# Four more column tiles of the input projection with tokens on the partitions, and PE transposes for the short convolution

## The chip, the cores and the metric

One core of one Trainium2 chip runs the program. The metric is the device time of one execution in microseconds (us), the median of several runs. The other numbers come from one profiled execution of the same program.

## What is computed

One layer of a decoder for 256 positions (T) and 2048 channels (D), in float32. From h = RMSNorm(x) one wide projection makes the inputs of three token mixers (attention, short convolution, state-space scan) and three merge gates:

```
h = rms_norm(x, g_mix)
... = split(h @ w_in)                       # q, k, v, gate_b, gate_c, u, z, xbc, dt, gm
y_a = nsa_mixer(...)                        # attention
y_b = gate_b * causal_depthwise_conv(gate_c * u, w)    # width 3 over positions
y_c = ssd_mixer(...)                        # state-space scan
gm = sigmoid(gm)
merged = gm[0] * y_a + gm[1] * y_b + gm[2] * y_c
x = x + merged @ w_o
x = x + relu(rms_norm(x) @ w_up) ** 2 @ w_down
x = x + (p @ w_ple) * sigmoid(rms_norm(x) @ w_ple_gate)
out = rms_norm(x, g_final)
```

The change touches y_b and its gate gm[1]: gate_c, u, gate_b and gm[1] are called cc, cu, cb and g1 in the kernel.

## The kernel before

The program is one long stream of weights. All weights stand in DRAM as 686 pieces of 128 x 1024 floats in the order of their use. For each piece SP issues a load into `raw` (6 buffers, line 75), ACT makes a rounded high part (line 87), DVE the low part by subtraction (line 88), both in `w` (4 buffers), and PE multiplies. The activations have a high and a low part too, so each product is three matmuls (high x high, high x low, low x high; `mm3`, lines 171 to 173).

A *unit* is 512 output columns: 8 pieces and 16 row tiles of 128, for all 256 tokens. `unit` (line 914) knows two kinds:

- kind A: tokens on the partitions of the result. The transposed activation tile (128 x 128) is the loaded operand, 512 columns of the weight stream past it. 2 token tiles x 16 row tiles x 3 = 96 matmuls of 512 columns. The two accumulators are [128 tokens, 512].
- kind B: channels on the partitions of the result. A 128 x 128 block of the weight is the loaded operand, the 256 tokens stream past it. 4 blocks x 16 x 3 = 192 matmuls of 256 columns. The accumulators are [128 channels, 2 blocks, 256 tokens].

In the loop over the units of the input projection (from line 964) `A = name in (...)` (line 979) picks the kind. After nine early units, four rounds j = 0 to 3 follow, one for each 512 channels: g0, q, x, z, g2, cc, cu, cb, g1. Of these q, x, z and g2 are of kind A, and g0, cc, cu, cb and g1 of kind B. ACT takes a finished unit out of PSUM (`evac`, line 950); only cu is taken by DVE, which multiplies it with cc on the way (line 1025) into `u`.

What the mixers do besides is cut into jobs: generators that issue a few instructions and then yield their estimated cost in ns. After each piece `side.run(BUDGET)` (line 946) lets the first four jobs in the list take at most one step each, out of a credit of 1200 ns a piece (capped at two pieces' worth). `lag()` gives up two such slots, so that data asked for by PE is ready when PE comes to it. The jobs of a round are `attn_job` (pushed after q), `ssd_job` (after x) and `sconv_job` (after cu); so the short convolution runs while cb and g1 are multiplied, and its last part, which needs g1, falls into the next round's g0, or, in the last round, into the output projection. PE runs its instructions in the order in which the planner of the program has put them; DVE and ACT likewise.

`sconv_job` before (line 893): per block of 128 channels one multiplication and two multiply-adds over shifted tokens (lines 897 to 900), into `yb`; a product with cb over 128 x 1024 (line 905); then `merge` (line 634) with g1 for all 256 tokens: twice a product (line 650) and an addition into `mg` (line 651) over 128 x 512. `mg[j]` is the merged activation, channels on the partitions, as the output projection wants it. `transpose4` (line 427) is four PE transposes of 128 x 128 blocks into one PSUM bank (line 431); attention and the scan use it already. PSUM has four banks for accumulators and four (`s`) for all side work.

The output projection follows (four units of kind A, named by n). `before_wo` splits `mg[c]` into `mTh` and `mTl` ahead of its chunk c; ahead of chunk 3 it lets all jobs come to their end (line 1071). Then come the MLP (16 units of kind B for w_up, 16 of kind A for w_down) and the gated embedding.

Of the kernel before, what the change touches and what calls it, by code (L numbers as in the profile page):

```python
# [21 lines left out]

# w_in column offsets
C_Q, C_KC, C_VC, C_KS, C_VS, C_KW, C_VW = 0, 2048, 2560, 3072, 3584, 4096, 4608
C_GN, C_CB, C_CC, C_CU, C_Z, C_X = 5120, 5168, 7216, 9264, 11312, 13360
C_B, C_C, C_DT, C_GM = 15408, 15920, 16432, 16464

# 1 / 10000 ** (2 i / 128) in float32
INV_FREQ = [
# [9 lines left out]

# 1 / (2 pi) in parts of 12 bits  # L40
TURN = [0.1591796875, -2.4750828742980957e-05, 6.421032594516873e-09,
# [6 lines left out]
def _units():  # L48
    """The column tiles of w_in in the order in which they are multiplied."""
    u = [("kc", 0, C_KC), ("ks", 0, C_KS), ("vs", 0, C_VS), ("kw", 0, C_KW), ("vw", 0, C_VW),  # L50
         ("vc", 0, C_VC), ("small", 0, 0), ("B", 0, C_B), ("C", 0, C_C)]
    for j in range(4):
        o = 512 * j
        u += [("g0", j, C_GM + o), ("q", j, C_Q + o), ("x", j, C_X + o), ("z", j, C_Z + o),
              ("g2", j, C_GM + 4096 + o), ("cc", j, C_CC + o), ("cu", j, C_CU + o),
              ("cb", j, C_CB + o), ("g1", j, C_GM + 2048 + o)]
    return u


def _pieces(name):  # L60
    """Widths of the pieces of a unit; the compression's first layer comes in between B's and C's."""
    return [128] * 2 if name == "small" else [512, 512, 128] * 4 if name in ("B", "C") else [512] * 8


class Stream:
    """Weights in order, two row tiles at a time: loads ahead, then high and low parts ahead of the products."""

# [24 lines left out]
    def get(self, i):  # L92
        """Piece i: [partition, part, row tile, column]."""
        self.convert(i + 1)
        return self.parts.pop(i)


class Side:
    """Work between the main products: each job does at most one step in a slot, a few jobs at a time."""

# [24 lines left out]
    def finish(self, *names):  # L125
        """Bring the named jobs to their end (all of them by default)."""
        while any(not names or n in names for _, n, _ in self.jobs):
            for job in self.jobs[:self.width]:
                self._step(job)


def _kern(tc, xT, xn, pT, pos, wbig, consts, colp, rowp, w2p, normg, gfin, cw, out):
# [50 lines left out]

    # ---- the stream of weights, in the order of their use
    units = _units()
# [19 lines left out]

    # ---- first loads; products on zeros until the first weights are there
    zero = tt([128, 512], name="zero")
# [48 lines left out]

    # ---- transposed activations x g in two parts (the token's factor comes after the first products)
    def aT(name):
# [11 lines left out]
    def rsqrt(dst, ss, n, count):  # L270
        """dst = (ss / count + EPS) ** -0.5 on [128, n]: a first guess from the exponent, three Newton steps."""
        v = sm([128, n], name="v")
# [84 lines left out]

    # ---- scratch in DRAM
    scr = {}
# [4 lines left out]

    # ---- kept over the token mixers
    # keys of a group: [second half, first half] of the selected branch, compressed, window branch
    kT = [kv([128, 2, 528], R32, name="kT") for _ in range(4)]
    vv = {(b, m): kv([128, 2, 512], R32, name="vv") for b in range(2) for m in range(2)}
    K_AT = {(0, 1): 0, (0, 0): 128, (1, 0): 272, (1, 1): 400}
    # compressed branch, 32 rows a part: values [high, high, low], weights [high, low, high]  # L370
    vcg = cst.tile([128, 4, 128], R32, name="vcg")
# [11 lines left out]

    # ---- the token's factor into the activations, once it is known
    hN = []
# [28 lines left out]

    # ---- side jobs
    def rope(dst, src, m):
        """dst, src: [128, 4, 2, 64]"""
        t = tt([128, 4, 2, 64], name="rt")
        V.tensor_tensor(dst, src, bc(cosT[:, m, None, None, :], [128, 4, 2, 64]), OP.mult)
        for h in range(2):  # L420
            V.tensor_tensor(t[:, :, h], src[:, :, 1 - h], bc(sinT[:, m, h, None, :], [128, 4, 64]), OP.mult)
        V.tensor_tensor(dst, dst, t, OP.add)
# [4 lines left out]
    def transpose4(src):  # L427
        """[128, 4 x 128] -> PSUM, each block transposed."""
        p = ps()
        for g in range(4):  # L430
            PE.transpose(p[:, sl(g)], src[:, sl(g)], ident)  # L431
        return p
# [23 lines left out]
    def conv_x(j, dst):  # L456
        """Causal depthwise convolution of the token-major columns kept in scr[j], and SiLU."""
        for hf in range(2):
# [19 lines left out]
    def conv_t(dst, accs, w):  # L478
        """The same with channels on the partitions, from PSUM: dst [128, 4, T], w [128, 4, taps + 1]."""
        for s in range(4):  # L480
# [82 lines left out]
    def blk_job(which):  # L563
        """Blocks of keys (values) with their position codes, transposed: per position [high 64 | low 64]."""
        pe = (pe_k, pe_v)[which]
# [15 lines left out]
    def phi_piece(which, c):  # L581
        """One quarter of the first layer of the compression: all products of the parts in one pass."""
        w = both()
# [50 lines left out]
    def merge(j, dst, a, b):  # L634
        """merged (transposed) += a * b, or a alone."""
        m = tuple(sorted(dst))
# [21 lines left out]
    def attn_job(j, ev):  # L658
# [18 lines left out]
        def pv(m, v, p):  # L677
            """ot[m] += v^T p, all heads at once."""
            if m not in ot:
# [10 lines left out]
        def scores(m, kind, hs):  # L690
            """Products of the queries of heads hs with the keys: one bank."""
            qh, ql = qq[m]
# [6 lines left out]
        def softmax(m, kind, hs, p, e):  # L699
            """e [128, rows, keys]: the gated weights of heads hs."""  # L700
            nr, nk = e.shape[1], e.shape[2]
# [23 lines left out]
        def spread(m, kind, u, p):  # L725
            """The transposed weights of two heads into [keys, part, head, token]."""
            if (m, kind) not in pt:
# [164 lines left out]

    def sconv_job(j, u):
        yb = b4([128, 4, T], name="yb")
        for s in range(4):
            w = scw[:, 4 * j + s]
            V.tensor_scalar(yb[:, s], u[:, s], w[:, 2:3], None, op0=OP.mult)
            for i in range(1, 3):
                V.scalar_tensor_tensor(yb[:, s, i:], u[:, s, :T - i], w[:, 2 - i:3 - i], yb[:, s, i:],
                                       op0=OP.mult, op1=OP.add)  # L900
            if s % 2:
                yield 1700
        while j not in cbe:
            yield None
        V.tensor_tensor(yb, yb, cbe[j], OP.mult)
        yield 1150
        while j not in sig1:
            yield None
        merged(j)
        merge(j, [0, 1], yb, sig1[j])  # L910
        yield 2400

    # ---- main products
    def unit(kind, lhs, accs, before=None, after=None, apart=False):
        """kind A: accs[m] [tokens, 512]; kind B: accs[s // 2] [128 columns, s % 2, tokens]."""
        for c in range(4):
# [3 lines left out]
            if apart and c == 3:  # L920
                # the last three pieces, the first token tile before the second
                w = [(2, 1, last3)] + [(3, hf, piece()) for hf in range(2)]
# [41 lines left out]
    for name, j, _ in units:  # L964
        if name == "small":
# [12 lines left out]
            continue  # L978
        A = name in ("kc", "ks", "vs", "kw", "vw", "q", "x", "z", "g2")
        early = name in ("kc", "ks", "vs", "kw", "vw")  # L980
# [40 lines left out]
        if name == "cu":  # L1021
            u = b4([128, 4, T], name="u")
            with tc.high_priority(offset=1000):
                for i in range(2):
                    V.tensor_tensor(u[:, sl(i, 2)], accs[i], cce[j][:, sl(i, 2)], OP.mult)
            side.push(sconv_job(j, u))
# [38 lines left out]

    # ---- output projection and residual
    mTs = {}
# [8 lines left out]
    def norm_T(n, gains, dst, parts):  # L1076
        """Sums of squares and the transposed, scaled activations of column tile n of x1."""
        h, lo = aT("h2h"), aT("h2l")
# [16 lines left out]
    for n in range(4):  # L1095
        accs = [acc(), acc()]
        # the slots of the merged activations come free chunk by chunk in the last tile
        unit("A", mTs, accs, before=before_wo if n == 0 else None,
# [5 lines left out]

    # ---- MLP, a quarter of the hidden features at a time; the square of the token's factor comes last
    h3, ss3 = {}, cst.tile([128, 2, 4], F32, name="ss3")
# [39 lines left out]

    # ---- per-layer embedding, gated
    pp = {}
# [70 lines left out]
class _Drain:  # L1219
    """Parts that jobs have yet to write: the jobs come to their end when a part is missing."""  # L1220

# [9 lines left out]
def _pack(w, c0, n=512):  # L1231
    """[K, N] -> pieces of [128, 2, 512] (partition, row tile, column)."""
    k = w.shape[0] // 256
# [80 lines left out]
```

## Time and profile before

| | |
|---|---|
| median of 3 runs | 2029.76 us (2028.83 to 2033.18) |
| profiled execution, first to last instruction | 2031.0 us |
| PE busy with matmuls | 2007.7 us, 99% |
| PE weight loads busy | 1821.4 us, 90% |
| DVE busy | 1324.7 us, 65% |
| ACT busy | 1022.5 us, 50% |

The profile gives no time of its own for the profiled execution other than this span; it lies between the fastest and the slowest of the three runs.

Line numbers are those of the kernel before. In the views an instruction's operands are named output<-inputs, where for PE the streamed operand comes first: `acc<-w,hNh` is kind A, `acc<-hNh,w` kind B. "x96" is a count. PE's durations overlap, because matmuls are pipelined: the duration of one is longer than the distance from its start to the next one's start. The times of PE are therefore best read from distances of starts, or from the length of a stretch and the number of matmuls in it.

### The profile page before, as it was taken

To read this page: it belongs to the slowest core of one execution; us is meant where nothing else is said; L and a number is where in the kernel's file an instruction comes from. 1 tells how busy PE (TensorE), PEld (TensorE's weight loads), DVE (VectorE), ACT (ScalarE), POOL (GpSimd) and SP (SyncE) were. 2 spreads that over 40 slices of the span, in tenths; PEclk is the share of its full clock that TensorE was granted. 3 is DMA by queue.
4 is the path that set the end of the run, shared out by engine and by line. 5 is a ranking of instruction groups with operands and counts; after the bars stand their busy time and mean duration, and the time that the engine had idled before them with its cause. 6 is when DMAs were issued, how large, how long until landed. Compare 5 with 4: busy or idle time off the path is not lost.

```text
span 2031.0 us, 31972 instructions
## 1 busy us (share of the span) xinstructions
PE 2007.7 (99%) x12693; PEld 1821.4 (90%) x12693; DVE 1324.7 (65%) x2075; ACT 1022.5 (50%) x1363; POOL 69.7 (3%) x93
## 2 busy tenths in 40 slices
PE   9999999999999999999999999999999999999997
PEld 7899988998799989998899889989988998998886
DVE  7877767766777668766887665555554555555665
ACT  7556556454555455454656454434443443445554
POOL 1000000000000000000000000000000000000011
PEclk9999999999999999999999999999999999999999
DMA  9556666655665566655675555555555555565553
GB/s 334 187 185 208 198 206 199 200 176 182 200 198 193 176 207 203 198 172 194 205 238 178 185 178 181 189 195 187 181 192 193 181 188 196 187 200 191 183 190 107
DMA packets 110277, 393.08 MB, mean 194 GB/s; under 512 B 12628, under 2 KB 13012, under 8 KB 110128
## 3 DMA queue, kind: packets, MB, share of 16 engines
q1 hardware_dynamic: 103552, 368.71, 55.4%
q0 software_dynamic: 6576, 22.34, 3.8%
q8 instruction: 99, 1.62, 0.3%
q14 instruction: 50, 0.41, 0.1%
HBM read 386.75 MB, written 4.25 MB: 193 GB/s over the span
## 4 chain that ended last, share of the span: by engine, by line
PE 51%; DVE 1%; issue 0%; ACT 0%; DMA 0%; POOLq 0%; POOL 0%; ACTq 0%
PE acc L173 17%; PE acc L171 17%; PE acc L172 17%; PE s L431 1%; DVE w L88 0%; DMA cv<-scrx 0%; PE s L171 0%; PE s L173 0%; PE s L172 0%; ACT w L87 0%; PE s L850 0%; ACT L720 0%; ACT scr L1190 0%; POOLq L1307 0%; DVE x L1188 0%
## 5 line engine op out<-in xcount | busy, mean ns | idle before, releaser
L88 DVE TENSOR_TENSOR w<-raw,w 128x1024 fp32r<-128x1024 f32 x686 | 840.1, 1226 | 605.5 <-ACT w L87 603.1
L87 ACT ACTIVATE w<-raw 128x1024 fp32r<-128x1024 f32 x686 | 726.0, 1059 | 850.5 <-PE acc L173 712.5
L171 PE MATMUL acc<-hNh,w 128*128 128x256 f32 x1488 | 423.6, 285 | 0.0
L173 PE MATMUL acc<-hNh,w 128*128 128x256 f32 x1488 | 421.0, 283 | 0.0
L172 PE MATMUL acc<-hNl,w 128*128 128x256 f32 x1488 | 420.9, 283 | 0.0
L171 PE MATMUL acc<-h2h,w 128*128 128x256 f32 x1024 | 290.0, 283 | 0.0
L173 PE MATMUL acc<-h2h,w 128*128 128x256 f32 x1024 | 289.8, 283 | 0.0
L172 PE MATMUL acc<-h2l,w 128*128 128x256 f32 x1024 | 289.8, 283 | 0.0
L172 PEld LDWEIGHTS acc<-hNl,w 128*128 128x128 f32 x1488 | 285.4, 192 | 0.7
L171 PEld LDWEIGHTS acc<-hNh,w 128*128 128x128 f32 x1488 | 285.3, 192 | 0.7
L173 PEld LDWEIGHTS acc<-hNh,w 128*128 128x128 f32 x1488 | 285.3, 192 | 0.0
L171 PE MATMUL acc<-w,hNh 128*128 128x512 f32 x512 | 201.3, 393 | 0.0
L171 PE MATMUL acc<-w,acth 128*128 128x512 f32 x512 | 199.8, 390 | 0.0
L173 PE MATMUL acc<-w,hNl 128*128 128x512 f32 x512 | 199.7, 390 | 0.0
L172 PE MATMUL acc<-w,hNh 128*128 128x512 f32 x512 | 199.5, 390 | 0.0
L173 PE MATMUL acc<-w,actl 128*128 128x512 f32 x512 | 199.3, 389 | 0.0
L172 PE MATMUL acc<-w,acth 128*128 128x512 f32 x512 | 199.3, 389 | 0.0
L172 PEld LDWEIGHTS acc<-h2l,w 128*128 128x128 f32 x1024 | 196.6, 192 | 0.1
L171 PEld LDWEIGHTS acc<-h2h,w 128*128 128x128 f32 x1024 | 196.6, 192 | 0.1
L173 PEld LDWEIGHTS acc<-h2h,w 128*128 128x128 f32 x1024 | 196.6, 192 | 0.0
L173 PEld LDWEIGHTS acc<-w,hNl 128*128 128x128 f32 x512 | 96.1, 188 | 20.6
L173 PEld LDWEIGHTS acc<-w,actl 128*128 128x128 f32 x512 | 96.1, 188 | 20.1
(354 smaller groups left out, 2427.9 us busy)
## 6 DMA issues: line engine op xcount, KB each, us to landing
raw<-wbig SPq DMA_DIRECT2D x686, 512.0 KB, 3.4
cv<-scrx POOLq DMA_DIRECT2D x16, 512.0 KB, 5.9
cw<-cw POOLq DMA_DIRECT2D x8, 512.0 KB, 4.7
E<-acsd POOLq DMA_DIRECT2D x16, 256.0 KB, 4.8
xb<-xn SPq DMA_DIRECT2D x4, 512.0 KB, 9.8
scrx<-ev POOLq DMA_DIRECT2D x4, 512.0 KB, 5.5
x<-xn SPq DMA_DIRECT2D x4, 512.0 KB, 7.1
out<-pp SPq DMA_DIRECT2D x8, 256.0 KB, 2.2
```

The source lines that it names most:

```text
L87: nc.scalar.activation(w[:, 0], s, AF.Copy)
L88: nc.vector.tensor_tensor(w[:, 1], s, w[:, 0].bitcast(F32), OP.subtract)
L171: PE.matmul(o, ah, bh, start=start, stop=False)
L172: PE.matmul(o, ah, bl, start=False, stop=False)
L173: PE.matmul(o, al, bh, start=False, stop=stop)
L431: PE.transpose(p[:, sl(g)], src[:, sl(g)], ident)
```

## The change

cc, cu, cb and g1 become units of kind A in all four rounds (16 units). Their results then have tokens on the partitions. `u` = cu x cc is made there, as two products over 128 x 512 from PSUM, as before. `sconv_job` then

- waits two slots, transposes u with PE, 4 blocks for each of the two token tiles, and has ACT copy them from PSUM into `uT`; the convolution into `yb` then runs as before, on `uT`;
- waits for both cb and g1, multiplies them with each other in place, 128 x 512 for each token tile, waits two slots, transposes the product with PE, and merges with `yb`: the transposed product is read from PSUM, and the merge is made by token tile.

The product of yb with cb over 128 x 1024 is gone.

The diff, without the removed comments and docstrings:

```
     def sconv_job(j, u):
+        uT = b4([128, 4, T], name="uT")
+        yield from lag()
+        for m in range(2):
+            p = transpose4(u[:, m])
+            S.activation(uT[:, :, sl(m)], p.rearrange("p (k t) -> p k t", k=4), AF.Copy)
+            yield 600
         yb = b4([128, 4, T], name="yb")
         for s in range(4):
             w = scw[:, 4 * j + s]
-            V.tensor_scalar(yb[:, s], u[:, s], w[:, 2:3], None, op0=OP.mult)
+            V.tensor_scalar(yb[:, s], uT[:, s], w[:, 2:3], None, op0=OP.mult)
             for i in range(1, 3):
-                V.scalar_tensor_tensor(yb[:, s, i:], u[:, s, :T - i], w[:, 2 - i:3 - i], yb[:, s, i:],
+                V.scalar_tensor_tensor(yb[:, s, i:], uT[:, s, :T - i], w[:, 2 - i:3 - i], yb[:, s, i:],
                                        op0=OP.mult, op1=OP.add)
             if s % 2:
                 yield 1700
-        while j not in cbe:
-            yield None
-        V.tensor_tensor(yb, yb, cbe[j], OP.mult)
-        yield 1150
-        while j not in sig1:
+        while j not in cbe or j not in sig1:
             yield None
         merged(j)
-        merge(j, [0, 1], yb, sig1[j])
-        yield 2400
+        for m in range(2):
+            t = cbe[j][:, m]
+            V.tensor_tensor(t, t, sig1[j][:, m], OP.mult)
+            yield 700
+            yield from lag()
+            p = transpose4(t)
+            merge(j, [m], p.rearrange("p (k t) -> p k t", k=4), yb[:, :, sl(m)])
+            yield 1500
...
-        A = name in ("kc", "ks", "vs", "kw", "vw", "q", "x", "z", "g2")
+        A = name not in ("vc", "B", "C", "g0")
...
         if name == "cu":
-            u = b4([128, 4, T], name="u")
+            u = b4([128, 2, 512], name="u")
             with tc.high_priority(offset=1000):
-                for i in range(2):
-                    V.tensor_tensor(u[:, sl(i, 2)], accs[i], cce[j][:, sl(i, 2)], OP.mult)
+                for m in range(2):
+                    V.tensor_tensor(u[:, m], accs[m], cce[j][:, m], OP.mult)
             side.push(sconv_job(j, u))
```

## Rows read from the trace of the kernel before

**Rows 1.** The page: the span, the engines with busy time, share of the span and number of instructions, and the chain of work that ended last, by engine.

```profile
span 2031.0 us, 31972 instructions
...
PE 2007.7 (99%) x12693; PEld 1821.4 (90%) x12693; DVE 1324.7 (65%) x2075; ACT 1022.5 (50%) x1363; POOL 69.7 (3%) x93
...
PE 51%; DVE 1%; issue 0%; ACT 0%; DMA 0%; POOLq 0%; POOL 0%; ACTq 0%
```

**Rows 2.** The view of waits for PE alone, whole span: who waited for what, us in total, times, longest in us.

```profile
PE s L431 <- DVE mx L718: 5.2, 5, 2.7
...
PE s L171 <- ACT e L720: 1.7, 4, 0.4
...
PE s L431 <- DVE y L885: 0.3, 1, 0.3
```

**Rows 3.** The view of waits for all engines: ACT's conversion of weights, the longest wait of all.

```profile
ACT w L87 <- PE acc L173: 712.5, 413, 3.2
```

**Rows 4.** The view of stretches: two units of kind A (w_down) and two of kind B (w_up) in the MLP, where PE has no side work. Columns: the stretch in us, its length, busy time and count of each engine, granted clock of PE, share of the DMA engines, GB/s. A stretch's count takes in one matmul that runs over its start (two in kind B).

```profile
1492.65:1514.41 21.76, 21.76 (x97) 18.02 (x96) 11.13 (x11) 8.49 (x8) 0.00 (x0) 1.00 0.59 194
1514.41:1536.17 21.76, 21.76 (x97) 18.02 (x96) 11.13 (x11) 8.49 (x8) 0.00 (x0) 1.00 0.59 193
1580.97:1604.01 23.04, 23.04 (x194) 23.04 (x193) 12.30 (x12) 10.59 (x13) 0.00 (x0) 1.00 0.55 183
1604.01:1627.05 23.04, 23.04 (x194) 23.04 (x193) 12.30 (x12) 10.60 (x13) 0.00 (x0) 1.00 0.55 184
```

**Rows 5.** The same view, unit by unit, columns as before: x and g2 of round 1; cc, cu, cb and g1 of round 1; g0, q and x of round 2; and the first unit of the output projection.

```profile
479.73:502.45 22.72, 22.72 (x105) 18.80 (x104) 14.76 (x18) 10.55 (x13) 0.00 (x0) 1.00 0.58 186
...
530.88:558.54 27.66, 27.26 (x136) 22.66 (x135) 23.43 (x65) 17.58 (x33) 2.27 (x3) 1.00 0.60 200
558.54:586.32 27.78, 27.78 (x222) 27.18 (x221) 21.72 (x37) 14.84 (x19) 2.04 (x3) 1.00 0.65 209
586.32:609.36 23.04, 23.04 (x194) 23.04 (x193) 16.92 (x21) 13.45 (x17) 0.00 (x0) 1.00 0.56 184
609.36:634.17 24.81, 24.81 (x210) 24.81 (x209) 16.91 (x27) 8.98 (x9) 2.03 (x3) 1.00 0.67 213
634.17:658.33 24.16, 24.16 (x201) 24.02 (x200) 19.66 (x40) 15.17 (x21) 0.00 (x0) 1.00 0.52 175
658.33:683.07 24.74, 24.74 (x210) 24.74 (x209) 13.65 (x15) 10.94 (x13) 0.00 (x0) 1.00 0.54 173
683.07:706.17 23.10, 23.10 (x105) 19.06 (x105) 16.10 (x28) 9.45 (x12) 0.00 (x0) 1.00 0.56 180
706.17:728.90 22.73, 22.73 (x105) 18.80 (x104) 14.76 (x18) 10.55 (x13) 0.00 (x0) 1.00 0.57 185
1105.08:1129.38 24.30, 24.30 (x117) 20.37 (x116) 17.11 (x24) 12.15 (x15) 0.55 (x1) 1.00 0.60 196
```

**Rows 6.** The view of line 431, the transposes: its matmuls by what they transpose, their number, and the duration of one in ns (least, median, most). `transpose4` issues four of them at a time.

```profile
L431 PE MATMUL s<-kb,e x96: 270/272/302, 297.0 to 1015.5; 128*128 128x128 f32 x96
...
L431 PE MATMUL s<-kb,x x64: 270/272/273, 1182.2 to 1931.2; 128*128 128x128 f32 x64
...
L431 PE MATMUL s<-kb,qr x32: 270/272/273, 270.0 to 946.5; 128*128 128x128 f32 x32
...
L431 PE MATMUL s<-kb,y x32: 270/272/328, 425.7 to 1134.3; 128*128 128x128 f32 x32
...
L431 PE MATMUL s<-kb,kr x24: 270/272/273, 71.6 to 115.3; 128*128 128x128 f32 x24
```

**Rows 7.** The timeline of PE in unit x of round 2, around four transposes in a row: start in us, duration in us.

```profile
719.78 0.60 PE L431 MATMUL s<-kb,qr 128*128 128x128 f32 x4
720.14 0.48 PE L171 MATMUL acc<-w,hNh 128*128 128x512 f32 x1
720.45 0.40 PE L172 MATMUL acc<-w,hNh 128*128 128x512 f32 x1
```

**Rows 8.** The view of groups by line and form, for the stretch from 456 to 1106 us (rounds 1 to 3): busy time in us, mean ns of one, idle time of the engine before them.

```profile
L163 ACT ACTIVATE pth<-s 128x512 fp32r<-128x512 f32 x18 | 10.5, 583 | 0.0
L855 DVE TENSOR_TENSOR y<-y,s 128x256 f32<-128x256 f32 x22 | 9.2, 417 | 0.3
...
L905 DVE TENSOR_TENSOR yb<-yb,ev 128x1024 f32<-128x1024 f32 x3 | 3.7, 1219 | 0.0
L650 DVE TENSOR_TENSOR mt<-yb,ev 128x512 f32<-128x512 f32 x5 | 3.4, 689 | 1.7 <-ACT ev L957 1.7
...
L651 DVE TENSOR_TENSOR mg<-mg,mt 128x512 f32<-128x512 f32 x4 | 2.8, 689 | 0.1
```

**Rows 9.** The timeline of the end of the last scan job, in the output projection: start in us, duration in us, and in brackets the idle time of the engine before it.

```profile
1133.21 0.69 DVE L885 TENSOR_TENSOR y<-y,ev 128x512 f32<-128x512 f32 x1
...
1133.96 0.66 PE L431 MATMUL s<-kb,y 128*128 128x128 f32 x4 [0.32 <-DVE y L885]
...
1134.96 0.68 DVE L646 TENSOR_TENSOR mg<-mg,s 128x512 f32<-128x512 f32 x1
...
1135.67 1.06 ACT L163 ACTIVATE mTh<-mg 128x1024 fp32r<-128x1024 f32 x1 [2.31 <-DVE mg L646]
...
1136.76 1.23 DVE L164 TENSOR_TENSOR mTl<-mg,mTh 128x1024 fp32r<-128x1024 f32 x1 [1.13 <-ACT mTh L163]
1136.77 0.40 PE L172 MATMUL acc<-w,mTh 128*128 128x512 f32 x1
```

## The prediction

> **What bounds the kernel now.** I began with the page. PE is busy for 99% of the span, and in the chain that ended last PE has 51% where every other engine has 1% or less [rows 1]. A busy PE is no proof, since durations of matmuls overlap, so I asked next who PE waits for. The largest wait between its first matmul and its last is 5.2 us in five places, transposes of attention weights that DVE had not got ready; then 1.7 us in four, and tenths [rows 2]. The view of all waits says the same from the other side: ACT, which makes the weights for PE, waits 712.5 us until PE gives back a weight buffer [rows 3]. So weights are ready ahead of PE, and neither DMA, ACT nor DVE sets the pace. The time is PE's instruction stream, and the question is what a unit of each kind costs there. That is read where nothing else runs on PE, in the MLP: a unit of kind A takes 21.76 us, one of kind B 23.04 us [rows 4]. Both stream 96 x 512 = 192 x 256 = 49,152 columns. Divided by the counts, a matmul of 512 columns takes 226.7 ns and one of 256 columns 120.0 ns, so two of the latter cost 13 ns more. The weight loads show why: in kind B they fill 23.04 of 23.04 us, in kind A 18.02 of 21.76 [rows 4]. The granted clock is 1.00 in all these stretches (the 2.4 GHz level).
>
> **The units that change kind.** Sixteen units (cc, cu, cb, g1 in four rounds) go from B to A: 16 x (23.04 - 21.76) = 20.5 us less. That the MLP's figures hold here too is seen in cu of round 1, which has no side work on PE: it takes 23.04 us, as in the MLP, though DVE works 16.92 us in it. And x, a unit of kind A with 8 transposes in it, takes 22.72 us [rows 5].
>
> **The new transposes.** Each round adds 4 groups of 4 transposes, 16 groups in all. One transpose is recorded with 272 ns, whatever it transposes [rows 6], but they overlap: four together take 0.60 us, and the next matmul starts 0.36 us after the first of them [rows 7]. What a group costs the stream is best read from unit x, which has two groups and nothing else: 22.72 - 21.76 = 0.96 us, 0.48 us a group [rows 4, 5]. In a unit of kind B a group costs less. g1 of round 1 has 4 transposes and 3 products of 512 columns and takes 1.12 us more than 23.04 [rows 5]; without 3 x 0.227 that leaves 0.44. The two groups for u fall into cb (now A), 2 x 0.48. The two for cb x g1 fall into the next g0 (B), 2 x 0.44, in the last round into the output projection (A), 2 x 0.48. Sum: 3 x 1.84 + 1.92 = 7.4 us; bounds 16 x 0.44 = 7.0 and 16 x 0.48 = 7.7. The Trainium skill has a rule that speaks against this (TensorE: Matmul & The Clock Gate, Part 4: PE-mode transpose): about 275 ns for a transpose in a kernel's context, by which the 64 would cost 17.6 us and the gain below would shrink to a fraction of a us. The recorded duration agrees with it; the distance of starts does not, and it is the distance that PE's stream pays.
>
> **Side work that now stands in units of kind A.** The matmuls of attention and scan in cc, cb and g1 stay, but around them the form changes. The sixteen in cb (two groups of the scan's) cost 24.81 - 23.04 = 1.77 us; in the first unit of the output projection, of kind A, two such groups and 3 products of 512 columns cost 24.30 - 21.76 = 2.54, without 3 x 0.227 that is 1.86. The seven in g1 cost 1.12, a like seven in q 23.10 - 21.76 = 1.34 [rows 4, 5]. So kind A pays 0.09 us more for two interruptions in the one case and 0.22 in the other. cc has 29 side matmuls, by their number some six interruptions, 0.3 to 0.7 us more by these two. A round: 0.09 + 0.22 + 0.3 to 0.7, together 2.4 to 4.0 us for four. From below 0, if the differences are the transitions between units and not the interruptions. I take 2.0, below the middle of what the rows give, because the 0.22 of q also holds a change of form at its start.
>
> **DVE and ACT.** Per round DVE loses one product of 1.22 us and four of 0.69 us (3.98), and gains two of 0.69 and eight over 256 elements, which in the nearest row (an addition from PSUM) take 0.42 each: 4.7 us [rows 8]. ACT gains two copies from PSUM of 0.58 us. That costs nothing as long as PE has work: in cb and g1 DVE is busy for 16.91 of 24.81 and 19.66 of 24.16 us, ACT for 8.98 and 15.17, and the later g0, where the second part goes, has 13.65 of 24.74 on DVE [rows 5]. A faster stream asks for a piece of weights every 2.72 instead of 2.88 us; the MLP's A units live on that without a wait [rows 4]. The products that make u are the same number over the same size.
>
> **New waits.** PE now waits for u, and for cb x g1, ahead of its transposes; behind a waiting transpose stands the whole stream, and all units with it. The cover is the two slots of `lag`, 2 x 2.7 us, against 0.7 us of DVE work for each tile. ACT's copy and DVE's merges wait for these transposes; behind them stand conversions of weights, and PE would miss those only when it has used up what is converted ahead, and the wait of ACT for free buffers [rows 3] says that it is ahead. I set the waits at 0. From above: the trace has 248 transposes, 62 groups of four [rows 6], and five waits for the maximum and one for y came to 5.5 us [rows 2], 0.09 us a group, 1.4 us for 16. From below: the order of side work shifts, and the five waits of 5.2 us could vanish. No DMA of a side job is added or moved.
>
> **The last round.** Its cb x g1 product, two groups of transposes and merges come into the output projection, where the scan's own end is tight. PE already waited 0.32 us for y there; mTh of the last chunk was ready at 1136.73 us and its matmul started at 1136.77 [rows 9]. Each us that this chain gets longer may cost a us. Before, the short convolution put 2.76 us of DVE work there, early; now it is 4.7 us, of which the second merge (1.7 us) falls among the scan's last steps. DVE is busy for 17.11 of 24.30 us in this unit [rows 5], so part of it goes into gaps. Bounds 0 and 2.0; I take 0.7, nearer to the gaps, since DVE sat idle for 1.13 us inside this very chain.
>
> **Sum.** -20.5 + 7.4 + 2.0 + 0.7 = -10.4 us on a span of 2031.0. That span is 1.2 us above the median of the runs and inside their spread, so I take the difference off the median: 2029.76 - 10.4 = 2019.4.
>
> **Rivals.**
> *The waits of attention go away.* All 5.2 us [rows 2]: 2014.2. For it: the order of the side work shifts. Against it: those transposes stand in z, which the change does not touch.
> *The new groups wait.* Place: PE ahead of the 16 new groups. The price of such a wait is known from attention, 5.2 / 5 = 1.04 us [rows 2]. If each group paid it: 16.6 us, 2036.0, slower than before. It decides from 0.40 us a group on (then the gain is inside 0.2%), and from 0.90 us on the kernel is slower by more than 0.2%. For it: DVE and ACT keep a fixed order, and a late instruction holds up all behind it. Against it: two slots of cover, and only 5 of all earlier groups waited so long. A part of it, or the output projection paying its full 2.0 us and more, gives 2021.5 to 2025.7.
> *Each transpose costs its recorded duration.* 64 x 0.272 = 17.4 instead of 7.4 us [rows 6]: 2029.4, no measurable change. Against it stands unit x [rows 5]. This is what the Trainium skill's figure above would give.
> *The change does not bring the faster form.* If the work of DVE, not PE's columns, set the pace of these units, the 20.5 us would not come, and the rest stays: 2039.9. For it: DVE is busy for 23.43 of 27.66 us in g2, of kind A. Against it: even there PE is busy for 27.26 [rows 5].
>
> **How the numbers follow.** A measurement of this kernel can tell about 0.2%, 4.1 us, from no change, so faster means under 2025.7 and slower over 2033.8. Chances: the sum within some 2 us 0.62; waits of attention gone 0.08; part of the new waits or a late output projection, up to 2025.7, 0.15; these three are faster, 0.85. Waits of 0.40 to 0.90 us a group 0.07 and transposes at full duration 0.03, the same, 0.10. Waits beyond that 0.03 and no faster form 0.02, slower, 0.05. The bounds of the terms give -20.5 + 7.0 + 0 + 0 - 5.2 = -18.7, 2011, and -20.5 + 7.7 + 4.0 + 2.0 + 1.4 = -5.4, 2024.4. All at one end at once is unlikely below, so I take 2012; above, the case of partial waits reaches to 2025.7, so I take 2025. With that less than 2 in 10 is left out: the 0.15 of the last four cases and the rims.
>
> **What the profile after would show.** The units cc, cu, cb and g1 with 96 matmuls of 512 columns each; cu without side work at 21.76 us; cb at about 1.3 us less for its form and 0.96 us more for two groups; weight loads no longer filling these units; g0 longer by 0.9 us; PE's waits still some 5 us, none on transposes of u or of the product; in the output projection the last `mg` about 1 us later. The prediction is wrong if line 431 gets waits of half a us in many places, if cu stays near 23 us, or if conversions of weights appear among PE's waits.

## The result, and the profile after

The changed kernel takes 2019.73 us (median of 4 runs, 2019.0 to 2020.36) where the kernel before takes 2029.49 (4 runs, 2028.83 to 2033.18): a ratio of 0.9949, 95% interval 0.9937 to 0.9961. It is 9.8 us faster; 10.4 had been forecast. The profiled spans differ by more, 2031.0 - 2017.0 = 14.0 us. Wherever a run's time and its span are both on record, the time is 1.8 to 2.5 us longer; so the profiled execution of the kernel before is one of about 2033 us, near the slowest of its runs and some 3.5 us above their median (the prediction compared span and run directly and had 1.2), and that of the changed kernel one of 2019.0, its fastest. What makes executions differ is one of the findings below.

The page of the changed kernel, as in [rows 1]: the span, and the engines' busy time, share and instructions.

```profile
span 2017.0 us, 29062 instructions
...
PE 1995.5 (99%) x11221; PEld 1747.1 (87%) x11221; DVE 1325.3 (66%) x2095; ACT 1024.3 (51%) x1369; POOL 69.5 (3%) x93
```

PE is still busy for 99%, with 1472 matmuls fewer: 16 x 96 went, 64 transposes came. DVE and ACT do what they did.

The view of stretches of the changed kernel, unit by unit as in [rows 5]: x, cc, cu, cb and g1 of round 1, g0 and q of round 2, and the first two units of the output projection.

```profile
476.27:499.00 22.73, 22.73 (x105) 18.80 (x104) 14.76 (x18) 10.54 (x13) 0.00 (x0) 1.00 0.55 186
552.20:578.99 26.79, 26.79 (x127) 22.08 (x125) 21.81 (x37) 14.81 (x19) 2.04 (x3) 1.00 0.64 215
578.99:600.75 21.76, 21.76 (x98) 18.02 (x96) 16.72 (x21) 13.61 (x17) 0.00 (x0) 1.00 0.58 196
600.75:625.31 24.56, 24.56 (x121) 20.59 (x120) 16.89 (x27) 9.94 (x11) 2.03 (x3) 1.00 0.58 190
625.31:648.27 22.96, 22.96 (x105) 18.98 (x103) 18.69 (x40) 15.04 (x21) 0.00 (x0) 1.00 0.61 210
648.27:674.56 26.29, 26.29 (x220) 26.10 (x219) 14.53 (x20) 11.33 (x13) 0.00 (x0) 1.00 0.53 175
674.56:696.93 22.37, 22.37 (x104) 18.51 (x102) 16.37 (x30) 9.33 (x12) 0.00 (x0) 1.00 0.52 172
...
1089.45:1114.69 25.24, 25.24 (x124) 21.16 (x123) 18.95 (x29) 11.23 (x14) 0.55 (x1) 1.00 0.54 175
1114.69:1137.71 23.02, 22.57 (x101) 18.19 (x100) 15.82 (x27) 10.55 (x13) 0.00 (x0) 1.00 0.56 181
```

Read it beside [rows 5]. cu, with no side work on PE, went from 23.04 to 21.76 us, the length of a unit of kind A in the MLP to the hundredth; its weight loads fill 18.02 us and no longer all of it. cc went from 27.78 to 26.79, g1 from 24.16 to 22.96. cb has two groups of transposes more and is still 0.25 us shorter. g0 and q together are 26.29 + 22.37 - 24.74 - 23.10 = 0.82 us longer: two groups in a unit of kind B (three products moved from q to g0 as well). x, untouched, is the same. The output projection's first two units are 25.24 + 23.02 - 24.30 - 22.87 = 1.09 us longer, with two groups in them.

The timeline of PE in cb of round 1, around the first group for u, and the view of PE's waits, both of the changed kernel.

```profile
609.84 0.60 PE L431 MATMUL s<-kb,u 128*128 128x128 f32 x4
610.19 0.48 PE L171 MATMUL acc<-w,hNh 128*128 128x512 f32 x1
```

```profile
PE s L431 <- DVE mx L718: 2.7, 3, 1.3
PE s L171 <- ACT e L720: 1.7, 4, 0.4
...
PE s L431 <- DVE y L885: 0.4, 1, 0.4
```

From the first of the four new transposes to the next matmul it is 0.35 us; attention's took 0.36 [rows 7]. PE's waits are those of before [rows 2], 2.5 us less of them on attention's maximum. None is on u or on the product of cb and g1.

The timeline of the changed kernel at the end of the last scan job, as in [rows 9]: the wait for y, and the last addition into `mg`.

```profile
1119.50 0.63 PE L431 MATMUL s<-kb,y 128*128 128x128 f32 x4 [0.45 <-DVE y L885]
...
1120.41 0.68 DVE L646 TENSOR_TENSOR mg<-mg,s 128x512 f32<-128x512 f32 x1
```

The last `mg` comes 1120.41 - 1089.45 = 30.96 us after the start of the output projection, before it was 1134.96 - 1105.08 = 29.88 [rows 5, 9]: 1.1 us later, of which 0.94 is the longer first unit. PE's wait for y grew from 0.32 to 0.45 us.

The groups by line and form for rounds 1 to 3 of the changed kernel (453 to 1090 us), as in [rows 8]: the merge from PSUM, the copies into uT, the product of cb and g1.

```profile
L650 DVE TENSOR_TENSOR mt<-s,yb 128x256 f32<-128x256 f32 x10 | 3.8, 418 | 2.2 <-PE s L431 2.2
L651 DVE TENSOR_TENSOR mg<-mg,mt 128x256 f32<-128x256 f32 x10 | 3.8, 418 | 0.0
L898 ACT ACTIVATE uT<-s 128x512 f32<-128x512 f32 x6 | 3.5, 580 | 0.0
L914 DVE TENSOR_TENSOR ev<-ev 128x512 f32<-128x512 f32 x4 | 2.8, 688 | 1.2 <-ACT ev L965 1.2
```

These are the prices that were taken from the nearest rows: 0.418 us for 256 elements from PSUM, 0.58 for ACT's copy, 0.69 for the product.

### The profile page after: what moved, and what is told of

Read it like the earlier page. It is cut to its first block, busy times and chain, and to the rows that moved or that the text cites. A ratio compares the mean times of both kernels' runs of the same rounds, so it can differ in the third digit from the quotient of the medians.

```text
span 2017.0 us, 29062 instructions
## 1 busy us (share of the span) xinstructions
PE 1995.5 (99%) x11221; PEld 1747.1 (87%) x11221; DVE 1325.3 (66%) x2095; ACT 1024.3 (51%) x1369; POOL 69.5 (3%) x93
## 4 chain that ended last, share of the span: by engine, by line
PE 51%; DVE 1%; issue 0%; ACT 0%; DMA 0%; POOLq 0%; POOL 0%; ACTq 0%
PE acc L171 17%; PE acc L173 17%; PE acc L172 17%; PE s L431 1%; DVE w L88 0%; DMA cv<-scrx 0%; PE s L171 0%; PE s L173 0%; PE s L172 0%; PE s L850 0%; ACT L720 0%; ACT scr L1198 0%; POOLq L1315 0%; DVE x L1196 0%; ACT w L87 0%
## 5 line engine op out<-in xcount | busy, mean ns | idle before, releaser
L171 PE MATMUL acc<-w,hNh 128*128 128x512 f32 x1024 | 403.9, 394 | 0.0
L173 PE MATMUL acc<-w,hNl 128*128 128x512 f32 x1024 | 399.3, 390 | 0.0
L172 PE MATMUL acc<-w,hNh 128*128 128x512 f32 x1024 | 399.2, 390 | 0.0
L173 PEld LDWEIGHTS acc<-w,hNl 128*128 128x128 f32 x1024 | 192.2, 188 | 41.2
L172 PEld LDWEIGHTS acc<-w,hNh 128*128 128x128 f32 x1024 | 192.5, 188 | 37.2
L171 PEld LDWEIGHTS acc<-w,hNh 128*128 128x128 f32 x1024 | 192.3, 188 | 37.2
L171 PE MATMUL acc<-hNh,w 128*128 128x256 f32 x464 | 132.4, 285 | 0.0
L173 PE MATMUL acc<-hNh,w 128*128 128x256 f32 x464 | 131.3, 283 | 0.0
L172 PE MATMUL acc<-hNl,w 128*128 128x256 f32 x464 | 131.2, 283 | 0.0
L172 PEld LDWEIGHTS acc<-w,acth 128*128 128x128 f32 x512 | 96.2, 188 | 19.6
```

The costliest lines, as they stand in the source:

```text
L171: PE.matmul(o, ah, bh, start=start, stop=False)
L172: PE.matmul(o, ah, bl, start=False, stop=False)
L173: PE.matmul(o, al, bh, start=False, stop=stop)
```

## The experiments

Times of a run are medians. The kernel before, run again beside the experiments, came to 2027.7 to 2035.6 us, with medians of 2029.05 to 2032.4 from batch to batch; the changed kernel was not run again beside them. So differences of a few us are read from the units of the profiles.

**1. No transposes.** In `sconv_job` of the changed kernel:

```
-            p = transpose4(u[:, m])
-            S.activation(uT[:, :, sl(m)], p.rearrange("p (k t) -> p k t", k=4), AF.Copy)
+            S.activation(uT[:, :, sl(m)], u[:, m].rearrange("p (k t) -> p k t", k=4), AF.Copy)
...
-            p = transpose4(t)
-            merge(j, [m], p.rearrange("p (k t) -> p k t", k=4), yb[:, :, sl(m)])
+            merge(j, [m], t.rearrange("p (k t) -> p k t", k=4), yb[:, :, sl(m)])
```

> The changed kernel without its 64 new transposes: ACT copies u straight into uT, and the merge reads the product of cb and g1 from SBUF. Left out: the swap of tokens and channels in the short convolution and its gate, so the values of y_b are others; all other work stays. Theory (each group of four costs PE's stream 0.44 to 0.48 us, and nothing waits for it): 7.4 us under the changed kernel's 2019.73, 2012.3. Rival 1 (each transpose costs its recorded 0.272 us): 17.4 us under, 2002.3. Rival 2 (part of the price of the new groups is waits): more than 8 us under, 2011 or less, and the units that lose their groups get shorter by more than 0.48 us a group.

Measured: 2016.21 us (2015.26 to 2016.71), 3.5 us less and not 7.4: by its time the theory missed. The view of stretches of this kernel, for z of round 1 and cb of round 1:

```profile
497.76:527.82 30.06, 26.30 (x120) 21.68 (x119) 19.10 (x47) 15.47 (x31) 3.12 (x5) 0.94 0.60 193
603.31:626.91 23.60, 23.60 (x114) 19.81 (x112) 16.98 (x27) 10.01 (x11) 2.04 (x3) 1.00 0.73 223
```

cb lost 0.96 us for its two groups, as expected, and over all units that had groups the loss is 7.2 us. But z of round 1, which the edit does not touch, takes 30.06 us instead of 25.51, and PE is busy for only 26.30 of them. The timeline there:

```profile
514.09 1.22 DVE L470 TENSOR_TENSOR cv<-cv,cw 128x1024 f32<-128x1024 f32 x1 [6.35 <-DMA cv<-scrx]
...
516.71 0.16 DVE L718 TENSOR_SCALAR mx<-mx 128x2 f32<-128x2 f32 x1
...
516.93 0.41 PE L431 MATMUL s<-kb,e 128*128 128x128 f32 x2 [1.10 <-DVE mx L718]
520.00 0.66 PE L431 MATMUL s<-kb,e 128*128 128x128 f32 x2 [2.66 <-DVE mx L718]
```

DVE stands for 6.35 us in the first product of the scan's convolution, whose data goes through DRAM and back; behind it, in DVE's fixed order, stands the maximum that attention's weights need, and PE waits for their transposes. The same wait is in z of round 1 of the kernel before, which took 28.42 us:

```profile
518.47 1.23 DVE L470 TENSOR_TENSOR cv<-cv,cw 128x1024 f32<-128x1024 f32 x1 [6.04 <-DMA cv<-scrx]
...
521.32 0.41 PE L431 MATMUL s<-kb,e 128*128 128x128 f32 x2 [0.78 <-DVE mx L718]
524.39 0.41 PE L431 MATMUL s<-kb,e 128*128 128x128 f32 x2 [2.66 <-DVE mx L718]
```

and, shorter, in the changed kernel:

```profile
512.15 1.23 DVE L470 TENSOR_TENSOR cv<-cv,cw 128x1024 f32<-128x1024 f32 x1 [3.16 <-DMA cv<-scrx]
...
518.06 0.41 PE L431 MATMUL s<-kb,e 128*128 128x128 f32 x2 [0.75 <-DVE mx L718]
```

Stretches of 2 us of run 1 show a second price, the granted clock (third column from the right):

```profile
515.00:517.00 2.00, 0.90 (x5) 0.47 (x4) 2.00 (x5) 0.10 (x1) 0.00 (x0) 1.00 0.38 51
...
519.00:521.00 2.00, 0.99 (x5) 1.03 (x6) 2.00 (x7) 1.03 (x5) 0.00 (x0) 0.61 0.51 180
521.00:523.00 2.00, 2.00 (x7) 1.61 (x7) 2.00 (x9) 1.21 (x2) 0.54 (x1) 0.54 0.46 160
```

After PE had been idle for most of 515.8 to 520.0 us, its clock was granted at the lower level (1.2 GHz) for a part of 519 to 523 us, and only 7 matmuls went through in 2 us where 11 do. Runs 8 to 11 follow this up.

**2. Each new transpose twice.** `for g in range(4 * times): PE.transpose(p[:, sl(g % 4)], src[:, sl(g % 4)], ident)` with `times=2` at the two new places.

> The changed kernel with each of its 64 new transposes issued twice in a row into the same bank; the computation is the same. Theory (the distance of starts counts, 0.109 us): 64 x 0.109 = 7.0 us over 2019.73, 2026.7, and cb longer by 2 x 0.44. Rival 1 (the recorded duration counts): 17.4 us over, 2037.1. Rival 2 (PE has slack at these places): under 3 us over.

Measured: 2025.56 us, 5.8 us more where the theory had 7.0. cb of round 1 in the view of stretches:

```profile
603.76:629.15 25.39, 25.39 (x130) 21.47 (x128) 16.88 (x27) 9.94 (x11) 2.04 (x3) 1.00 0.54 177
```

25.39 - 24.56 = 0.83 us for eight more transposes, 0.104 us each, as expected. So PE's stream pays the distance of starts; the recorded 0.272 us would have made 2.2 us of it. That rival falls.

**3 and 4. Each half alone.** First only cc and cu change kind, then only cb and g1:

```
-        A = name not in ("vc", "B", "C", "g0")
+        A = name not in ("vc", "B", "C", "g0", "cb", "g1")     # 3, with the old product and merge
+        A = name not in ("vc", "B", "C", "g0", "cc", "cu")     # 4, with the old u, uT = u
```

> One half of the change: cc and cu of kind A with u transposed, cb and g1 of kind B with the old product and merge. Theory (terms add): cc 0.99 and cu 1.28 us less a round, as the changed kernel's profile has them, 9.1 us in four rounds; 8 groups of transposes in a unit of kind B, 8 x 0.44 = 3.5 us more; 5.6 us under the kernel before, 2023.9. Rival (the two halves help each other, by one shared wait or by the buffers): this half alone gives 3 us or less, 2026.5 or more.

> The other half: cb and g1 of kind A, multiplied with each other and transposed for the merge, cc and cu of kind B with u made with channels on the partitions as before. Theory (terms add): cb 1.2 and g1 1.2 us less a round, 9.6 us in four; 8 groups, 0.82 us a round in g0 and q and 1.1 in the output projection, 3.6 us more; 6.0 us under the kernel before, 2023.5, and with the other half 11.6 us. Rival (the last round's tail and the merge from PSUM eat it): 3 us or less, 2026.5 or more.

Measured: 2022.96 us (2022.15 to 2023.47) and 2026.46 us (2022.54 to 2027.29). The first half is as expected. The second half's median misses, and its runs lie in two bunches, near 2023 and near 2027; the profiled span, 2021.3 us, belongs to the first bunch and its units are those expected. cb and g1 of round 1:

```profile
604.85:628.47 23.62, 23.62 (x114) 19.81 (x113) 16.82 (x27) 8.96 (x9) 2.04 (x3) 1.00 0.68 223
628.47:651.45 22.98, 22.98 (x105) 18.97 (x103) 18.67 (x40) 15.04 (x21) 0.00 (x0) 1.00 0.55 183
```

They are 1.2 us shorter each, and g0 and q are 0.84 us longer together. That the second bunch is the wait in z is not shown, as only one execution has a trace.

**5. No slots of cover.** Both `yield from lag()` in `sconv_job` taken out.

> The changed kernel without the two slots of cover ahead of its 16 groups of transposes: they are asked for right after the products that they turn; the computation is the same. Theory (the new waits are 0 because of the two slots): without them PE waits for DVE at the 8 groups of cb x g1, about as long as attention's waits, 0.5 to 1.0 us each, and not for u, which is ready before the first slot ends: 4 to 8 us over 2019.73, about 2025. Rival (the planner of the order already puts the transposes where their data is ready, and the slots do nothing): within 1.5 us of 2019.73.

Measured: 2019.99 us, the same as with them; the theory missed and the rival held. The timeline of this kernel at cb of round 1:

```profile
600.33 1.28 DVE L1031 TENSOR_TENSOR u<-acc,ev 128x512 f32<-128x512 f32 x2
...
604.10 0.66 PE L431 MATMUL s<-kb,u 128*128 128x128 f32 x4
```

The first group for u comes 3.5 us into cb, with the slots 9.1 us; u is ready 1.0 us into cb in both. The theory spoke of the groups for cb x g1; the first of round 1, in the next g0:

```profile
648.53 0.69 DVE L913 TENSOR_TENSOR ev<-ev 128x512 f32<-128x512 f32 x1 [0.68 <-ACT ev L963]
...
653.75 0.60 PE L431 MATMUL s<-kb,ev 128*128 128x128 f32 x4
```

The product is ready at 649.22 us, and its transposes come 4.5 us later. So without the slots, too, PE's transposes are put behind their data; whether the steps of the jobs or the planner does that was not tested.

**6. Kind A for w_up too.** On top of the changed kernel; w_up's units become "A", and the squared activations are turned in a side job:

```
+        def act_turn(a, n, ts):
+            yield from lag()
+            h, lo = b4([128, 4, T], R32, name="acth"), b4([128, 4, T], R32, name="actl")
+            for m in range(2):
+                p = transpose4(ts[m])
+                split(h[:, :, sl(m)], lo[:, :, sl(m)], p.rearrange("p (k t) -> p k t", k=4))
...
-                unit("B", h2, accs)
+                unit("A", h2, accs)
```

> The same exchange at 16 more units, on top of the changed kernel: the MLP's w_up of kind A, its squared activations transposed by PE in groups of four, two groups a unit, split from PSUM; the computation is the same. Theory (a unit of kind A with two groups costs 21.76 + 0.97 = 22.73 us against 23.04, and the two slots cover the waits): 16 x 0.31 = 5.0 us under 2019.73, 2014.7. Rival (the last unit's activations come late for w_down, or ACT and DVE, which split from PSUM, hold up the weights): each of the four changes from w_up to w_down waits 1.2 us or more, and nothing is gained, 2019.7 or more.

Measured: 2015.5 us (2014.31 to 2016.84), 4.2 us less. Two stretches of this kernel, a unit of w_up and the first of w_down, which now holds the last unit's transposes:

```profile
1252.57:1275.29 22.72, 22.72 (x105) 18.81 (x104) 12.30 (x12) 10.53 (x13) 0.00 (x0) 1.00 0.54 185
1275.29:1298.02 22.73, 22.73 (x105) 18.80 (x104) 12.51 (x13) 10.06 (x12) 0.00 (x0) 1.00 0.54 186
```

22.72 us, as unit x [rows 5], against 23.04 [rows 4]; PE has no wait in either.

**7. The last round's gate as before.** `... and not (j == 3 and name in ("cb", "g1"))`, with the old product and merge in that round.

> The changed kernel, but in the last round cb and g1 stay of kind B with the old product and merge, so that no transposes come into the output projection. Read from the units of the profile. Theory (nothing but columns and groups): cb and g1 of that round 1.2 us longer each, the first two units of the output projection together 1.0 to 1.1 us shorter, mg of the last scan in time as before. Rival (the tail pays for DVE's extra work as well): the output projection gets shorter by 1.7 us or more.

Measured (one run, 2020.28 us): cb and g1 of the last round are 1.1 and 1.2 us longer, and the first two units of the output projection 1.1 us shorter than in the changed kernel:

```profile
1092.25:1116.55 24.30, 24.30 (x117) 20.38 (x116) 17.10 (x24) 12.17 (x15) 0.55 (x1) 1.00 0.57 190
1116.55:1139.40 22.85, 22.54 (x101) 18.24 (x100) 15.71 (x26) 10.56 (x13) 0.00 (x0) 1.00 0.54 179
```

That is two groups at 0.48 and 0.15 us more; DVE's extra work there costs next to nothing.

**8 to 11. The wait in z moved away.** In `conv_x`, DVE's first product of a round goes four slots back (`lag(2)` gives up four; the first expectation counts five), behind the conversion of weights that is due then (`ws.last`, which the stream of weights now keeps):

```
                 yield 0
-                V.tensor_tensor(u, u, w, OP.mult)
+                if hf == 0 and m == 0:
+                    yield from lag(2)
+                    with tc.issue_after(getattr(ws.last, "ins", ws.last)):
+                        V.tensor_tensor(u, u, w, OP.mult)
+                else:
+                    V.tensor_tensor(u, u, w, OP.mult)
```

This was run with the kernel before, with the changed kernel, with run 6 and with run 1.

> The kernel before, with one instruction moved: in each round DVE's first product of the scan's convolution (line 470), which waits for data that goes through DRAM and back, is put five slots later in DVE's order, behind a conversion of weights that is due then; the computation is the same. It tests what sets the spread of unit z, the only unit whose length differs from profile to profile. Theory (DVE stands in that wait, attention's maximum is late behind it, and PE waits for it): DVE's waits for cv fall from 24 us to under 5, PE's waits for line 718 from 5.2 us to under 1, all four z between 24.0 and 25.0 us, and the time 2 to 4 us under the kernel before's. Rival (PE's waits in z come from attention's own chain): z and the time unchanged within 1 us.

> The changed kernel with the same one instruction moved. With z out of the comparison the change alone is left. Theory (the sum of the units' differences in the two profiles, z left out): 11 to 12 us under the run above, a ratio of 0.9943. Rival (what the change gives depends on the waits in z): 9 us or less under it, or 14 or more.

> The changed kernel with w_up of kind A (as in the run of that name) and the same one instruction moved. Theory (terms add): 4.5 to 5.0 us under the run above. Rival (they get in each other's way): 3 us or less under it.

> The changed kernel without its 64 new transposes (left out as in the first experiment, so the values of y_b are others) and with the scan's one instruction moved. The first experiment gained 3.5 us where 7.4 were expected, while the units that lost their groups got shorter by 7.2 us and z of round 1 longer by 4.6. Theory (that z was the same wait for data through DRAM, in an unlucky place): with z out of the way the transposes' price shows in full, 7.2 us under the changed kernel with the moved instruction, 2008.1, and all four z within 0.2 us of 26.2. Rival (without the transposes something else waits in z): z of round 1 stays longer than the others by 2 us or more, and the time is 2010 or more.

| | us, median | lowest to highest | runs |
|---|---|---|---|
| kernel before, moved | 2027.29 | 2026.81 to 2027.87 | 11 |
| changed kernel, moved | 2015.33 | 2015.19 to 2015.57 | 5 |
| and w_up of kind A | 2010.01 | 2009.5 to 2010.17 | 4 |
| changed kernel, no transposes, moved | 2007.81 | 2007.39 to 2008.15 | 4 |

The spread of several us is gone. The four z of the kernel before with the move, in the view of stretches:

```profile
278.44:304.60 26.16, 26.14 (x131) 21.78 (x130) 19.24 (x53) 16.94 (x33) 3.93 (x6) 1.00 0.73 230
500.95:527.23 26.28, 26.28 (x130) 21.81 (x129) 19.27 (x53) 16.93 (x33) 3.89 (x6) 1.00 0.72 230
723.53:749.69 26.16, 26.14 (x130) 21.78 (x129) 19.23 (x53) 16.93 (x33) 3.90 (x6) 1.00 0.73 230
946.05:972.33 26.28, 26.28 (x130) 21.80 (x129) 19.27 (x53) 16.92 (x33) 3.90 (x6) 1.00 0.73 229
```

PE is busy throughout; its waits for line 718 are gone altogether. The four z of runs 9 and 11 are as long, 26.15 to 26.28 us. Three details were expected otherwise: the z are 26.2 us and not 24 to 25, because attention gets further in them (33 side matmuls instead of 22, which later units no longer have), DVE still waits 12.4 us for data from DRAM, in later products, with no wait of PE for line 718 behind them; and the time is 5.1 us under the kernel before's 2032.4 beside it, where 2 to 4 were expected. The move also brought in a new wait of PE, for a conversion of weights in the second unit of the output projection, from the view of PE's waits of run 8:

```profile
PE acc L172 <- DVE w L88: 0.8, 1, 0.8
```

That unit takes 23.70 us in run 8, against 22.87 in the kernel before and 23.01 in run 9. Without the transposes, too, z of round 1 is no longer than the others, and cb is as short as in run 1:

```profile
496.69:522.97 26.28, 26.28 (x131) 21.82 (x130) 19.26 (x53) 16.91 (x33) 3.88 (x6) 1.00 0.71 231
...
597.34:620.94 23.60, 23.60 (x114) 19.80 (x113) 16.97 (x27) 10.01 (x11) 2.03 (x3) 1.00 0.67 223
```

So with the move the change gives 2027.29 - 2015.33 = 12.0 us. Of these, 0.8 is the wait just named, which run 8 has and run 9 has not: the change by itself is worth some 11.2 us, and the two first profiles with z left out say the same, 14.0 - 2.6 = 11.4. The transposes cost 2015.33 - 2007.81 = 7.5 us; run 11 was made on another chip than runs 8 to 10, but units without transposes agree (cu 21.76 us in both), and by the units alone the difference is 7.2 us. w_up of kind A gives another 5.3 us, slightly more than expected. The third row of the table is 0.9896 of the kernel before run beside it, interval 0.9883 to 0.9910.

## Why the prediction came out

*What bounds the kernel, and the form.* Right. PE's instruction stream sets the time, and 512 columns in one matmul are cheaper than in two. cu shows it alone (23.04 to 21.76), and kernel before and run 11, both with z out of the way, differ by 2027.29 - 2007.81 = 19.5 us for the sixteen units with their side work, 0.8 of it the wait in run 8. The rival that DVE's work would keep the units at their old length is refuted: cc has 21.81 us of DVE's work in 26.79 and became 0.99 us shorter. What the prediction gave as the reason, weight loads that fill a unit of kind B, stays open. From the page of the kernel before:

```profile
L172 PEld LDWEIGHTS acc<-h2l,w 128*128 128x128 f32 x1024 | 196.6, 192 | 0.1
```

A load is recorded with 192 ns. At a distance of 120 ns such records overlap and fill the stretch, whatever sets the distance, just as those of the matmuls do; no run tells the two apart.

*The transposes.* Right: 7.4 forecast, 7.2 by the units of runs 1 and 11 and 7.5 by the medians of runs 9 and 11, and the price is the distance of starts. The Trainium skill's figure (TensorE: Matmul & The Clock Gate, Part 4: PE-mode transpose), about 275 ns and given there for bfloat16, is what the trace records for one, 272; as a price in a dense stream it does not hold here, 0.104 us in run 2.

*Side work in units of kind A.* Right: 2.0 us forecast; cc, cb and g1 of the profiles give 0.29 + 0.07 + 0.08 a round, 1.8 in all. The runs with z out of the way give 20.5 - 19.5 = 1.0, and 1.8 once the wait of 0.8 us in run 8 is taken out. Within the term g1's share is 0.08 where q's row had suggested 0.22, of which the prediction itself suspected a part to be q's change of form.

*New waits at 0.* Right in size: the view of waits has none on the new groups. Wrong in its reason: without the two slots there is none either (run 5).

*The last round.* 0.7 us forecast, 1.09 - 0.96 = 0.13 measured, 0.15 by run 7. The last `mg` did come 1.1 us later, as forecast, but nearly all of that is the first unit's own length with its two groups; PE's wait for y grew by only 0.13 us.

*The sum.* With what the units of the profiles show, it is -20.5 + 7.2 + 1.8 + 0.1 = -11.4, and that is the difference of the profiles with z left out. The forecast's -10.4 was 1.0 us short: 0.6 too dear in the last round, 0.2 each in the transposes and the side work. That it lies within 0.6 us of the 9.8 of the medians is partly luck, because the medians hold something that no term contained: the wait in z, which differs from execution to execution (25.2 to 28.4 us for z of the kernel before, 24.9 to 26.0 for the changed one). The same changed kernel stands 9.8 us under the four runs of the kernel before that were made with it, and would stand 12.7 under the median of 2032.4 of the fifteen beside runs 8 to 10. In the two profiled executions z together is 2.6 us shorter, hence 14.0 us there. The rival *waits of attention go away* named this wait but took its row for something fixed; in the profiled executions half of it went (5.2 to 2.7 us), in z, which the change does not touch, and in run 1 it is 5.2 us again.

## What to carry to other kernels

When PE's stream is the bound, count what each form of a product costs there from the start of one matmul to the start of the next, in a stretch without side work, and add the interruptions as the difference of two stretches; durations of single matmuls or transposes mislead by a factor of about two (272 against 104 ns for a transpose). A swap of partitions and columns can pay for its transposes: a unit of kind A with eight of them (22.73 us) was shorter here than one of kind B with none (23.04 us). Before comparing kernels to a few us, look for the one unit that differs from profile to profile and take its cause out of both: here one instruction, put where its data has arrived, made the spread of the kernel before several times smaller (6.9 us in fifteen runs, 1.1 in eleven). And look for what the moved kernel waits for instead: 0.8 of the 12.0 us was such a wait.

## What was not expected of the hardware

A pause of PE can cost more than its own length. In z of round 1 DVE waited for data that goes through DRAM and back, 6.0 us in the kernel before and 6.4 in run 1, and PE was idle for 0.78 + 2.66 and 1.10 + 2.66 us around the same two transposes. In run 1 the granted clock then fell, 0.61 and 0.54 on average over two stretches of 2 us, 7 matmuls ran where 11 do, and PE was busy for 26.30 us in the unit:

```profile
502.46:530.88 28.42, 24.98 (x119) 20.58 (x118) 17.93 (x44) 14.16 (x30) 3.12 (x5) 1.00 0.63 193
```

This is the same unit of the kernel before: 24.98 us busy, at a clock of 1.00. The lower clock thus cost about 1.3 us on top of 3.8 us of idle time. Why it came in the one execution and not in the other, whose pause was only 0.3 us shorter, no run here shows.
